# Hybrid gated-attention layer: second branch's factors one stage on, branch sums on VectorE, recurrent values in blocks of 512 columns

## The chip, the cores and the metric

One core of a Trainium2 chip runs the whole layer. The metric is the device time of one execution in microseconds. Engines are named as the profile names them: PE is TensorE (PEld its weight loads), DVE is VectorE, ACT is ScalarE, POOL is GpSimd, SP is SyncE, which here issues transfers.

## The reference

The layer takes x (1024 tokens by 1024 channels, float32) and a conditioning vector c. In short:

```python
mod = silu(c) @ ada_w + ada_b                      # shift, scale, gate
h = rms_norm(x) * (1 + scale) + shift
hq, hf, hi, hz, gq, gk, gv, gz, ga, mg = split(h @ w_in)
y_h = rms_norm(attention(silu(hq), k(hf), hi, log f(hf)), whole width) * silu(hz)
y_g = rms_norm(attention(gq, gk, gv, log_sigmoid(ga @ alpha)/16), per head) * silu(gz)
u_h, u_g = y_h @ w_branch[0], y_g @ w_branch[1]
merged = sigmoid(mg[0]) * u_h + sigmoid(mg[1]) * u_g
out = rms_norm(x + gate * (merged @ w_out))
```

`attention` is causal gated linear attention: a state per head that decays by a gate for each channel. The recurrent branch (HGRN, y_h) has 8 heads of 128 channels, the other (GLA, y_g) 4 heads with 128 key and 256 value channels.

## The kernel before

**Precision.** Every large float32 product is made of three matmuls of a faster type: an operand is split into a high half (cast on ScalarE, L193, L1163, L1182) and a low half (operand less high half on VectorE, L196, L1164, L1183), and high x high, high x low and low x high are summed in PSUM.

**Projections.** A list of jobs runs one after the other (`Stream.go`, L738). `Feat` (L461) makes 128 features of all tokens: 8 steps of 6 matmuls with 512 moving columns. `Vblk` (L480) makes the values of 256 columns: the tokens' tile of h is the stationary operand and 256 columns of weights move, 192 matmuls in 16 steps. The GLA heads come first, then the 8 recurrent heads; before every second of these stands a `Vblk` for two heads. Weights of the next jobs are loaded and split ahead (`ahead`, L721) as far as the 46 buffers of 4 KB a partition allow; the splitting ahead is tried at the fourth step of a job alone.

**Tracks.** After each step, `weave` (L749) advances two queues of side work: `side`, with the attention of one head after the other (L528, which holds TensorE, ScalarE and VectorE steps), and `back`, with preparations for the products. Each entry yields how many steps it wants to wait. On each engine, instructions run in the order in which they stand there.

**Gate side.** `gate_side` (L899) loads the third part of ada_w in eight pieces, sums them on VectorE, each times a value of c (L907, L909), and spreads the sum over the partitions with four full-precision matmuls (L916, L917). It stands in `side`, ahead of the first recurrent head's attention.

**Products.** The last stages (L1287) make four products of 1024 x 1024 x 1024, b = 0 to 3: the two merge gates' columns (b = 0: gate 1, b = 1: gate 0), then the GLA branch (b = 2) and the recurrent branch (b = 3). Each is made block by block with seven instead of eight block products, in the order p = 1, 2, 5, 6, 3, 7, 4 ("groups" below: 48 matmuls each, four pairs of output tiles with 12). That takes sums and differences of blocks, the factors, of h, y_g and y_h. `factors` (L1067) loads four blocks of the activations from memory, subtracts (L1087), and stores the factors to memory, twice. For y_h the blocks are first multiplied by the reciprocal norm (L1081), and all seven are stored. `build` (L1153) loads a group's factor and splits it, `prep_duo` (L1179) does so with the weights of two pairs, two tiles ahead (L1292). ScalarE and VectorE take the results out of PSUM (L1220, L1225, L1229).

**Merging.** `put_gate1` stores the sigmoid of gate 1 to memory (L1316), and `load_gate1` brings it back; `put_t1` multiplies it with u_g. `put_m` (L1334) multiplies gate 0 with u_h and adds the GLA part:

```python
nc.vector.tensor_mul(g, g, ap)
nc.gpsimd.dma_start(g, gate1[d][:, sl], accum_op=ALU.add)
```

The second line is a transfer that adds, issued from POOL. `make_m` (L1346) then splits the sum, leaving the last two halves for later. `OutBlk` (L995) makes the output projection, 16 blocks of 24 matmuls, each taken out of PSUM by VectorE (L1030).

## Time and profile before

| what | us |
|---|---|
| three runs | 1292.81, 1295.80, 1296.76 (median 1295.8) |
| the profiled execution | 1292.4, its span 1290.7 |
| PE busy | 1227.4 |
| DVE busy | 791.7 |
| ACT busy | 505.9 |
| projections and attention | 126 to 844 of the span |
| products b = 0, 1, 2, 3 | 844 to 1190 |
| output projection | 1190 to 1291 |

Times of one profiled execution are counted from the start of its span. A row "x waits for y" gives the time in which an engine had nothing to do and what ended it. Busy times of overlapping instructions are not added twice in a window. A granted clock of 1.00 is TensorE at full speed; 0.50 is half.

### The profile page before, as it was taken

How to read it: one execution, taken by the hardware profiler on the slowest of the kernel's cores; microseconds unless marked ns; L12 is line 12 of the kernel's file. 1: busy time of each engine (PE TensorE's matmuls, PEld its weight loads, DVE VectorE, ACT ScalarE, POOL GpSimd, SP SyncE). 2: the span in 40 equal slices, each digit the busy share in tenths (PEclk: the TensorE clock that was granted, in tenths of full speed). 3: DMA queues.
4: the chain of work that ended last, by engine and by line, in shares of the span. 5: the costliest groups of instructions: out<-in, count | busy, mean ns of one | idle time of the engine just before them, and what ended most of it. 6: DMA issues, size and time to landing. Idle time of an engine off the chain costs nothing. (4 is left out here: it accounts for less than half of the span.)

```text
span 1290.7 us, 21711 instructions
## 1 busy us (share of the span) xinstructions
PE 1227.4 (95%) x8987; PEld 1025.7 (79%) x8987; DVE 791.7 (61%) x1223; ACT 505.9 (39%) x754; POOL 158.9 (12%) x254
## 2 busy tenths in 40 slices
PE   4899999999999989999999999989889999998997
PEld 3767889888898868888987898868678877786785
DVE  5746445877857488677547735676742547547543
ACT  4556522333232423243233222456445555444222
POOL 6500000212113011120110110101210000002000
PEclk9799999999999999999999999999999999998999
DMA  9723342546537375642120221236977546668402
GB/s 281 280 98 99 114 141 89 196 132 212 173 102 253 117 243 184 221 157 58 51 66 18 83 83 49 84 106 226 344 261 269 165 161 199 182 185 212 153 34 98
DMA packets 138485, 199.30 MB, mean 154 GB/s; under 512 B 8075, under 2 KB 102337, under 8 KB 138386
## 3 DMA queue, kind: packets, MB, share of 16 engines
q1 hardware_dynamic: 121314, 144.21, 35.6%
q0 software_dynamic: 17024, 53.70, 11.9%
q8 instruction: 70, 1.15, 0.4%
q14 instruction: 29, 0.24, 0.1%
q10 hardware_dynamic: 48, 0.01, 0.0%
HBM read 140.21 MB, written 53.48 MB: 150 GB/s over the span
## 5 line engine op out<-in xcount | busy, mean ns | idle before, releaser
L455 PE MATMUL pd<-b,b 128*128 128x512 f32 x1632 | 395.9, 396 | 0.0
L455 PEld LDWEIGHTS pd<-b,b 128*128 128x128 f32 x1632 | 301.0, 188 | 62.9 <-issue 0.7
L1242 PE MATMUL pd<-b,b 128*128 128x512 f32 x912 | 223.1, 398 | 17.7 <-ACT b L1182 5.1
L1242 PEld LDWEIGHTS pd<-b,b 128*128 128x128 f32 x912 | 171.4, 191 | 60.8 <-ACT b L1220 7.0
L196 DVE TENSOR_TENSOR b<-b,b 128x1024 fp32r<-128x1024 f32 (+1 forms) x95 | 105.4, 1122 | 81.9 <-ACT b L193 53.5
L514 PE MATMUL pd<-b,b 128*128 128x256 f32 x512 | 150.0, 293 | 0.0
L193 ACT CAST b<-b 128x1024 fp32r<-128x1024 f32 (+1 forms) x95 | 84.7, 905 | 157.4 <-DMA b<-b 25.4
L516 PE MATMUL pd<-b,b 128*128 128x256 f32 x512 | 145.2, 284 | 0.0
L515 PE MATMUL pd<-b,b 128*128 128x256 f32 x512 | 145.0, 283 | 0.0
L1242 PE MATMUL sc_ps<-b,b 128*128 128x512 f32 x432 | 106.8, 393 | 0.1
L1183 DVE TENSOR_TENSOR b<-b,b 128x1024 fp32r<-128x1024 f32 x56 | 67.7, 1219 | 51.5 <-ACT b L1182 34.9
L514 PEld LDWEIGHTS pd<-b,b 128*128 128x128 f32 x512 | 98.1, 192 | 1.3
L515 PEld LDWEIGHTS pd<-b,b 128*128 128x128 f32 x512 | 98.1, 192 | 0.7
L516 PEld LDWEIGHTS pd<-b,b 128*128 128x128 f32 x512 | 98.0, 191 | 0.1
L1242 PEld LDWEIGHTS sc_ps<-b,b 128*128 128x128 f32 x432 | 80.7, 189 | 18.3 <-DVE b L1330 0.5
L1182 ACT CAST b<-b 128x1024 fp32r<-128x1024 f32 x56 | 58.1, 1049 | 41.1 <-DMA gate<-b 8.4
L1164 DVE TENSOR_TENSOR b<-b,b 128x1024 fp32r<-128x1024 f32 x36 | 43.7, 1220 | 35.7 <-ACT b L1163 23.2
L1124 POOL DMA_DIRECT2D ws<-b x64 | 34.7, 543 | 165.5 <-DVE b L1119 70.8
L1163 ACT CAST b<-b 128x1024 fp32r<-128x1024 f32 x36 | 37.7, 1049 | 41.5 <-PE pd L1242 10.1
L702 PE MATMUL pm<-scT,b 128*128 128x128 f32 x256 | 46.9, 275 | 0.0
L634 DVE TENSOR_TENSOR b<-b,tot 128x512 f32<-128x512 f32 x36 | 24.9, 691 | 34.3 <-PE sc_ps L615 15.0
L704 PE MATMUL pm<-b,b 128*128 128x128 f32 x224 | 43.3, 275 | 0.0
(241 smaller groups left out, 1772.9 us busy)
## 6 DMA issues: line engine op xcount, KB each, us to landing
b<-in_w_in_dram SPq DMA_DIRECT2D x66, 512.0 KB, 4.6
ws<-b POOLq DMA_DIRECT2D x64, 256.0 KB, 4.1
b<-ws SPq DMA_DIRECT2D x32, 512.0 KB, 4.4
b<-in_x_dram SPq DMA_DIRECT2D x16, 512.0 KB, 5.7
b<-in_ada_w_dram SPq DMA_DIRECT2D x32, 256.0 KB, 6.0
b<-in_w_branch_dram SPq DMA_DIRECT2D x16, 512.0 KB, 4.9
b<-h SPq DMA_DIRECT2D x14, 512.0 KB, 3.9
b<-yg SPq DMA_DIRECT2D x14, 512.0 KB, 4.6
```

What stands on the lines that cost most here:

```text
L193: i = nc.scalar.copy(hi, src)
L196: (eng or nc.vector).tensor_sub(lo, src, hi.bitcast(F32))
L455: nc.tensor.matmul(ps[0:w, th * 512:(th + 1) * 512], a[:, k, 0:w], b[:, th * 512:(th + 1) * 512], start=(k == 0 and n == 0), stop=(k == KT ...
L514: nc.tensor.matmul(o, lh, hi[:, k % 4, :], start=(k == 0), stop=False)
L515: nc.tensor.matmul(o, lh, lo[:, k % 4, :], start=False, stop=False)
L516: nc.tensor.matmul(o, ll, hi[:, k % 4, :], start=False, stop=(k == KT - 1))
L702: nc.tensor.matmul(o, vch(ch)[:, vh * P:(vh + 1) * P], scT[:, ch, :], start=True, stop=(ch == 0))
L704: nc.tensor.matmul(o, state(ch)[:, vh * P:(vh + 1) * P], q[:, ch * P:(ch + 1) * P], start=False, stop=True)
L1164: nc.vector.tensor_sub(lo, src, hi.bitcast(F32))
L1182: nc.scalar.copy(hi, t)
L1183: nc.vector.tensor_sub(lo, t, hi.bitcast(F32))
L1242: nc.tensor.matmul(o, a[:, sl], c, start=(p in (1, 5) and kt == 0 and n == 0), stop=(kt == 3 and n == 2), skip_group_check=True)
```

## The change

It has five parts.

1. The values of the recurrent heads are made by a new job, `Vblk2`, in two blocks of 512 columns for four heads each. The block stands behind the projections hq and hf of its first head, and that head's attention is started when half of the block is done (`middle`). A head's attention asks for the values when it first needs them (`v = v()`). Weights are split ahead at every second step from the fourth.
2. `gate_side` goes to the rear track, 4 steps after the first block, so behind the weight sums and the GLA factors that stand there, and leaves 3 steps between its last sum and its matmuls.
3. The factors of y_h are begun after p = 2 of b = 1, not at the end of the last head's attention, and their loads are issued from POOL, not SP.
4. `put_m` adds on VectorE, and `make_m` leaves one half for later, not two.
5. `factors` and `weight_sums` wait until 12 buffers are free, not 8 and 6.

```diff
+    class Vblk2:
+        raws, parts = 4, 8
...
+        def run(self):
+            v = [S.get([2, 512]) for _ in range(4)]
+            for g in range(4):
+                if g == 2:
+                    self.middle()
+                ps = dtile()
+                for i in range(2):
+                    t = 2 * g + i
+                    o = ps[:, i * 512:(i + 1) * 512]
+                    for k in range(KT):
+                        hi, lo = self.wt[k // 2]
+                        lh, ll = h_hi[k][:, t * P:(t + 1) * P], h_lo[k][:, t * P:(t + 1) * P]
+                        nc.tensor.matmul(o, lh, hi[:, k % 2, :], start=(k == 0), stop=False)
+                        nc.tensor.matmul(o, lh, lo[:, k % 2, :], start=False, stop=False)
+                        nc.tensor.matmul(o, ll, hi[:, k % 2, :], start=False, stop=(k == KT - 1))
+                        if k % 2:
+                            yield
+                nc.scalar.copy(v[g].rearrange("p a b -> p (a b)"), ps)
...
-                    if u == 3:
+                    if u >= 3 and u % 2:
                         self.ahead(i, loads, preps)
...
             yield 1
+        yield 3
         gate_b[0] = S.get([D])
...
-            stream.back.append([factors(yh_d, f_h, rst), 1])
+            rst_h[0] = rst
+
+    def hgrn_v(h):
+        def done(v):
+            h_state[("v", h // 4)] = v
+            if h == 0:
+                stream.back.append([gate_side(), 4])
+        J.append(Vblk2(C_HI + h * P, done, lambda: start_side(hgrn_attention(h), 4)))
...
-            while len(S.free_list) < 8:
+            while len(S.free_list) < 12:
...
-                nc.sync.dma_start(y[b], part_of(acts, int(b[0]) - 1, int(b[1]) - 1, kk))
+                (nc.sync if mul is None else nc.gpsimd).dma_start(y[b], part_of(acts, int(b[0]) - 1, int(b[1]) - 1, kk))
...
-        while len(S.free_list) < 6:
+        while len(S.free_list) < 12:
...
-        nc.gpsimd.dma_start(g, gate1[d][:, sl], accum_op=ALU.add)
+        nc.vector.tensor_add(g, g, gate1[d][:, sl])
...
-            after(3, p, i, lambda: make_m(2))
+            after(3, p, i, lambda: make_m(1))
...
+    after(1, 2, 3, lambda: stream.back.append([factors(yh_d, f_h, rst_h[0]), 1]))
```

What this moves on the engines, at three places. First TensorE in the values of the recurrent heads; the first block before, and the second block now. Behind the arrow stands first the operand that moves, a half of the weights, and then the stationary one, a tile of h (b_140 and b_148 are the high and low half of one).

```order
L514 MATMUL pd_4782<-b_4507,b_140 128x256
L515 MATMUL pd_4782<-b_4508,b_140 128x256
L516 MATMUL pd_4782<-b_4507,b_148 128x256
L514 MATMUL pd_4782<-b_4507,b_141 128x256
L515 MATMUL pd_4782<-b_4508,b_141 128x256
```

```order
L557 MATMUL pd_5970<-b_5736,b_140 128x512
L558 MATMUL pd_5970<-b_5737,b_140 128x512
L559 MATMUL pd_5970<-b_5736,b_148 128x512
L557 MATMUL pd_5970<-b_5736,b_141 128x512
L558 MATMUL pd_5970<-b_5737,b_141 128x512
```

The same three matmuls for each tile of h now move 512 columns, and there are half as many of them: 384, not 768.

Second, TensorE around the gate side's four matmuls (to pm), before and now. The scores of a head's first step go to sc_ps, the projections' to pd; b_4210 and b_6466 are the sum over the eight pieces.

```order
L455 MATMUL pd_4300<-b_145,b_4247 128x512 x2
L916 MATMUL pm_4308<-b_4210,ones 128x512
L917 MATMUL pm_4308<-b_4211,ones 128x512
L916 MATMUL pm_4312<-b_4210,ones 128x512
L917 MATMUL pm_4312<-b_4211,ones 128x512
L554 MATMUL sc_ps<-xb,b_4101 32x80 x32
```

```order
L597 MATMUL sc_ps<-xb,b_6522 32x80 x32
L455 MATMUL pd_6530<-b_145,b_6478 128x512 x2
L455 MATMUL pd_6530<-b_153,b_6478 128x512 x2
L455 MATMUL pd_6530<-b_145,b_6479 128x512 x2
L963 MATMUL pm_6630<-b_6466,ones 128x512
L964 MATMUL pm_6630<-b_6467,ones 128x512
L963 MATMUL pm_6634<-b_6466,ones 128x512
L964 MATMUL pm_6634<-b_6467,ones 128x512
```

Before, they stand ahead of the first recurrent head's first scores; now behind those of the sixth, six matmuls later.

Third, VectorE in group p = 3 of b = 3, before and now. L1229 (now L1280) takes a block product out of PSUM, L1337 (now L1388) multiplies with gate 0, L1391 is the new addition, L196 makes the low half of the merged sum, L1183 (now L1234) that of weights.

```order
L1229 TENSOR_TENSOR b_10019<-b_10019,pd_7872 128x512
L1183 TENSOR_TENSOR b_10136<-b_10046,b_10135 128x1024
L1337 TENSOR_TENSOR b_8753<-b_8753,b_10019 128x512
L1229 TENSOR_TENSOR b_10019<-b_10019,sc_ps 128x512
L1337 TENSOR_TENSOR b_8769<-b_8769,b_10019 128x512
L1229 TENSOR_TENSOR b_10060<-b_10060,pd_7872 128x512
L1337 TENSOR_TENSOR b_8793<-b_8793,b_10060 128x512
L196 TENSOR_TENSOR b_9898<-b_8753,b_9897 128x512
```

```order
L1388 TENSOR_TENSOR b_8331<-b_8331,b_9639 128x512
L1234 TENSOR_TENSOR b_9754<-b_9666,b_9753 128x1024
L1391 TENSOR_TENSOR b_8331<-b_8331,b_8555 128x512
L1280 TENSOR_TENSOR b_9639<-b_9639,sc_ps 128x512
L196 TENSOR_TENSOR b_9490<-b_8331,b_9489 128x512
L1388 TENSOR_TENSOR b_8345<-b_8345,b_9639 128x512
L1280 TENSOR_TENSOR b_9680<-b_9680,pd_7441 128x512
L1391 TENSOR_TENSOR b_8345<-b_8345,b_8601 128x512
L1388 TENSOR_TENSOR b_8365<-b_8365,b_9680 128x512
L1391 TENSOR_TENSOR b_8365<-b_8365,b_8651 128x512
```

Each multiplication has an addition behind it, and the low half of the sum (L196) follows one multiplication later; before, three multiplications lay between.

More of the change, by code (lines that the diff above doesn't have):

```diff
@@ L522, in run, with __init__, load, prep @@
             self.done(v)
+    class Vblk2:
+        raws, parts = 4, 8
+        def __init__(self, col, done, middle):
+            self.col, self.done, self.middle = col, done, middle
+        def load(self):
+            self.raw = []
+            for kk in range(4):
+                b = S.get([2, 512])
+                nc.sync.dma_start(b, w_in2[kk * 256:(kk + 1) * 256, self.col:self.col + 512].rearrange(
+                    "(k p) f -> p k f", p=P))
+                self.raw.append(b)
+        def prep(self):
+            self.wt = []
+            for b in self.raw:
+                self.wt.append(split(b))
+                S.free(b)
+        def run(self):
[16 more added lines that the diff above has]
+                nc.scalar.copy(v[g].rearrange("p a b -> p (a b)"), ps)
+            for hi, lo in self.wt:
+                S.free(hi, lo)
+            self.done(v)
     def rhs_h(k):
```

27 lines of the change are left out of this document (13 added, 14 removed).

## The prediction

> **What bounds the kernel now.** I read the page first, then the busy time by stage, then what TensorE waited for, and last the timeline around the longest of those waits. The page says which engine is full:
>
> ```profile
> span 1290.7 us, 21711 instructions
> ...
> PE 1227.4 (95%) x8987; PEld 1025.7 (79%) x8987; DVE 791.7 (61%) x1223; ACT 505.9 (39%) x754; POOL 158.9 (12%) x254
> ```
>
> TensorE is busy for 95% of the span. So only two things shorten the run: TensorE instructions that cost less, and waits of TensorE that go. The last five stages of the program, by windows (length, then busy time and instructions of PE, PEld, DVE, ACT and POOL, then granted clock, DMA share and GB/s; they are the products b = 0, 1, 2, 3 and the output):
>
> ```profile
> 844.00:942.70 98.70, 90.32 (x569) 71.99 (x568) 66.91 (x88) 52.54 (x78) 16.63 (x28) 0.98 0.66 227
> 942.70:1023.50 80.80, 77.22 (x337) 62.56 (x336) 35.16 (x35) 40.94 (x56) 2.92 (x6) 1.00 0.69 231
> 1023.50:1103.00 79.50, 77.83 (x337) 62.46 (x336) 47.63 (x52) 40.07 (x50) 0.00 (x0) 1.00 0.58 185
> 1103.00:1190.20 87.20, 80.46 (x338) 64.29 (x338) 51.35 (x61) 42.11 (x57) 12.03 (x14) 0.96 0.67 186
> 1190.20:1290.70 100.50, 89.60 (x385) 72.79 (x383) 44.06 (x74) 26.88 (x56) 1.72 (x2) 0.96 0.29 101
> ```
>
> Stages b = 1, 2 and 3 hold the same 336 matmuls and take 80.8, 79.5 and 87.2 us. The difference is waiting. The list of TensorE's waits names it (us in total, times, longest):
>
> ```profile
> PE pd L1242 <- ACT b L1182: 5.1, 1, 5.1
> PE pd L1242 <- ACT b L1220: 4.8, 3, 2.9
> PE pm L259 <- DVE scT L251: 4.0, 2, 2.2
> PE pm L916 <- DVE b L909: 3.6, 1, 3.6
> PE pm L818 <- DVE b L196: 3.5, 5, 0.8
> PE pd L1242 <- DVE b L1229: 3.4, 2, 2.6
> PE pd L1025 <- DVE xb L1030: 3.1, 2, 2.3
> ```
>
> Of these seven, L259 lies in the start and L818 in the attention, which the change leaves as they are. The other five, 20.0 us, stand where the change works.
>
> **Values in blocks of 512 columns.** Four blocks of 192 matmuls with 256 moving columns become two blocks of 192 with 512. The timeline gives the pitch of both: a run of 111 matmuls of 512 columns, and two of 256 columns between whose starts 45 steps lie:
>
> ```profile
> 450.20 25.33 PE L455 MATMUL pd<-b,b 128*128 128x512 f32 x111
> ...
> 526.77 0.28 PE L516 MATMUL pd<-b,b 128*128 128x256 f32 x1
> ...
> 532.17 0.28 PE L516 MATMUL pd<-b,b 128*128 128x256 f32 x1
> ```
>
> 25.33 / 111 is 0.228 us, the last one's tail included; (532.17 - 526.77) / 45 is 0.120 us. Before, 768 x 0.120 = 92.2 us; now 384 x 0.228 = 87.6 us. That is **-4.6 us** on the path. The Trainium skill, in "TensorE: Matmul & The Clock Gate", section "Back-to-back issue gap", gives an isolated warm matmul its columns over 2.4 GHz and 2.5 ns besides. By that page the 384 matmuls saved are worth 384 x 2.5 ns = 1.0 us, an estimate, and the sum below would be 3.6 us smaller; the two pitches above do not agree with it, since twice 0.120 is 0.012 us more than 0.228. What could take from the 4.6: the four weight tiles of a block are cast and subtracted four steps before it starts, while VectorE also serves a head. Each tile lasts TensorE six matmuls, 1.4 us, so a late tile costs about that; I allow 2 us for both blocks at the far end, and take nothing.
>
> **The gate side moved.** Before, the eight accumulations of the gate bias (L909) run ahead of the first recurrent head, and TensorE meets the four full-precision matmuls (L916, L917) before the last accumulation is there. The timeline row, and then the windows around four places with their granted clock (third value from the end):
>
> ```profile
> 479.09 1.43 PE L916 MATMUL pm<-b,ones 128*128 128x512 f32 x2 [3.56 <-DVE b L909]
> ```
>
> ```profile
> 475.50:490.00 14.50, 10.94 (x76) 4.92 (x76) 11.09 (x15) 3.14 (x5) 1.62 (x3) 0.65 0.39 128
> 926.60:933.50 6.90, 3.94 (x11) 2.54 (x10) 5.29 (x6) 1.76 (x3) 1.63 (x3) 0.77 1.12 353
> 1161.70:1173.00 11.30, 6.16 (x15) 4.36 (x15) 8.92 (x11) 5.54 (x7) 1.72 (x2) 0.70 0.99 265
> 1207.40:1214.00 6.60, 4.28 (x12) 3.23 (x12) 3.05 (x5) 1.45 (x4) 0.00 (x0) 0.74 0.08 32
> ```
>
> A wait costs twice here: TensorE idles 3.56 us, and the clock granted over the 14.5 us around it is 0.65, so (1 - 0.65) x 14.5 = 5.1 us of matmul work is lost as well. Now the accumulations stand in the rear track, spread over two jobs of the sixth head, three steps ahead of the matmuls, and in TensorE's order the matmuls stand behind the sixth head's first scores, whose own vector operations come after the last accumulation in VectorE's order. When TensorE gets there, the accumulation is done. So **-8.7 us**; at the far end 0, if another operation is late there. The 9 transfers and 8 vector operations are the same ones, and the first recurrent head no longer waits behind them.
>
> **The second branch's factors, one stage on.** Before, they run from p = 6 of b = 0 into p = 1 of b = 1. The windows of p = 3, 7, 4 of b = 0 and p = 1 of b = 1, and then of p = 5 and 6 of b = 1, where they will stand (each holds 48 matmuls, which take 48 x 0.228 = 10.9 us):
>
> ```profile
> 904.00:914.90 10.90, 10.90 (x50) 9.03 (x49) 10.11 (x10) 6.73 (x9) 3.22 (x6) 1.00 1.01 327
> 914.90:929.70 14.80, 11.37 (x50) 8.81 (x48) 8.89 (x11) 5.00 (x7) 3.72 (x7) 1.00 0.98 345
> 929.70:942.70 13.00, 12.67 (x48) 9.95 (x49) 5.55 (x6) 5.31 (x8) 3.56 (x8) 0.87 0.92 334
> 942.70:957.80 15.10, 11.52 (x49) 8.86 (x48) 9.52 (x9) 5.44 (x7) 2.92 (x6) 1.00 0.84 297
> ...
> 968.80:979.80 11.00, 11.00 (x50) 8.96 (x49) 3.58 (x3) 5.73 (x9) 0.00 (x0) 1.00 0.58 199
> 979.80:990.70 10.90, 10.90 (x49) 8.90 (x48) 2.45 (x2) 6.32 (x9) 0.00 (x0) 1.00 0.96 333
> ```
>
> The second to fourth rows lose 3.9, 2.1 and 4.2 us, **10.2 us** together, with the DMA engines full (shares of 0.84 to 1.01). VectorE, which makes the low halves of TensorE's operands in order, stands behind the factors' loads:
>
> ```profile
> 938.20 1.23 DVE L1081 TENSOR_TENSOR b<-b,b 128x1024 f32<-128x1024 f32 x1 [5.23 <-DMA b<-yh]
> ```
>
> In the new place VectorE is busy 3 us of 11 instead of 9 to 10, no factor is built for b = 1, and gates are not stored to memory. But the bytes come along: 8 loads and 14 stores of 512 KB are 11.5 MB, or 33 us of the DMA engines at the 345 GB/s of the second row, over seven groups; and p = 6 of b = 1 stands at 333 GB/s already. So some of the stall goes with them. Between nothing and the same 10.2 us again I take half, 5.1, since the operands are prepared two weight tiles, one group, ahead, and the load on VectorE is a third. Net **-5.1 us**. The rear end is +2 (the same stall and some more, as the last head's attention, now two steps later, then lies wholly in b = 0); the near end -10.2.
>
> These loads also go from SP's queue to POOL's. POOL waits there for VectorE's results with its stores, but the four loads of a half are issued before its first store. How quickly POOL's transfers land beside SP's, for the factors themselves (KB each, median us):
>
> ```profile
> fh<-b POOLq DMA_DIRECT2D x14, 512.0 KB, 6.2
> b<-fh SPq DMA_DIRECT2D x14, 512.0 KB, 4.2
> ```
>
> Two microseconds more is inside the six steps (8 us) that are left between load and use. A wider threshold of free buffers (12, not 8 or 6) delays the weight sums, but in the order in which the program is written out they end in the middle of the values of heads 4 to 7, before the products begin; I cost it at nothing; the cover is the projections of the four heads that follow, and without it the first products would wait for their weights.
>
> **Branches added on VectorE.** Before, VectorE multiplies (L1337), POOL issues an adding DMA (L1340), and ScalarE's cast of the sum (L193) waits for the landing. The windows of p = 3, 7, 4 of b = 3, ScalarE's wait, TensorE's wait in the output stage, and an addition of the size of the new one:
>
> ```profile
> 1148.00:1158.90 10.90, 10.90 (x50) 9.03 (x49) 8.57 (x11) 2.37 (x4) 2.53 (x3) 1.00 0.56 152
> 1158.90:1178.10 19.20, 14.06 (x50) 10.57 (x49) 11.55 (x16) 7.67 (x11) 1.76 (x4) 0.82 0.86 229
> 1178.10:1190.20 12.10, 11.17 (x50) 8.94 (x49) 11.55 (x15) 6.26 (x8) 4.28 (x5) 1.00 0.82 185
> ```
>
> ```profile
> 1163.18 0.62 ACT L193 CAST b<-b 128x512 fp32r<-128x512 f32 x1 [8.02 <-DMA b<-b]
> ```
>
> ```profile
> 1209.91 0.59 PE L1025 MATMUL pd<-b,b 128*128 128x512 f32 x1 [2.32 <-DVE xb L1030]
> ```
>
> ```profile
> L1032 DVE TENSOR_TENSOR b<-b,xb 128x512 f32<-128x512 f32 x16 | 11.1, 692 | 0.5
> ```
>
> ScalarE stands 8.02 us for one landing, and behind it in its order stand the casts of the weights (L1182) for which TensorE then waits 5.1 us. The group takes 19.2 us instead of 10.9: **8.3 us**, half clock included. The 2.32 us in the output stage come from the same landings, since the last casts hold VectorE's queue, and the clock of 0.74 over 6.6 us adds 1.7: **4.0 us**. Together 12.3 us go. In exchange VectorE does 16 additions, 11.1 us, 12 of them (8.3 us) in these three groups. There it was busy 8.57 + 11.55 + 11.55 = 31.7 us; now it needs 40.0, and three unhindered groups of TensorE last 32.7. So VectorE becomes the late engine at the end, by 7.3 us. TensorE notices that only where it needs something from VectorE: the last weights' low halves, and in the output stage the eviction of the third block, 17 us after the stage begins (1209.91 - 2.32 - 1190.20). Before, that eviction came 2.32 us too late, with VectorE idle in between for the landings. Of the 7.3 us I take 4 as felt: net **-8.3 us**, between -12.3 and, with the 7.3 felt whole and 4.0 of half clock again, -1.0.
>
> **The sum.** -4.6 - 8.7 - 5.1 - 8.3 = -26.7 us. The profiled execution took 1292.4 us, its span 1290.7 and 1.7 around it; it would come to 1265.7. It lies 3.4 us under the median of the three runs, 1295.8, so against that the forecast is **1269 us**. All near ends give -35.8 (1260), all rear ends -2.6 + 0 + 2 - 1.0 = -1.6 (1294).
>
> **Rivals.** *The stall moves with the factors.* The 11.5 MB find the DMA engines full in b = 1, where p = 6 shows 333 GB/s, and TensorE waits for weights there as it did before: the 5.1 us won are not won and 5 more are lost. For it speaks the DMA share of 0.96; against it, that the group with that share took 10.9 us. -26.7 + 5.1 + 5 = -16.6, or 1279 us. Chance 0.13.
>
> *The gate's wait only moves.* If VectorE is behind when TensorE reaches L916's successor, the 8.7 us are paid again: 1278 us. VectorE's order speaks against it. This is also how the change would fail to do what it says. Chance 0.07.
>
> *Slower: the loads on POOL.* VectorE stands in order before each half's first multiplication. If POOL's loads come so late that VectorE waits longer than TensorE's one prepared group, 10.9 us, the rest is lost twice. To lose the 26.7 us, each half must come 10.9 + 13.4 = 24.3 us late; at 30 us late the time is 1269 + 2 x 19.1 = 1307 us. The longest such wait in the trace is 5.23 us. The Trainium skill, in "SBUF — State Buffer", section "SBUF: two separate sides", says that a DMA from POOL's queue cannot write its descriptors while VectorE runs an operation that takes both memory ports, and so appears blocked; that rule speaks against this part of the change. The 6.2 against 4.2 us above bound what it does here so far. Chance 0.03.
>
> **How the numbers follow.** The forecast holds 0.77: its own range is 1260 to 1277. The range 1257 to 1284 takes in the first two rivals and 3 us of spread below. A measurement of this kernel can tell about 0.3%, 3.9 us, from no change. Faster by more than that needs 1291.9 or less: the forecast and both first rivals, and most of what they give together (-8.0 us): 0.94. Within 0.3%: 0.03. Slower: 0.03, the last rival.
>
> **What would show it.** Right: 512-column matmuls for all recurrent values, at 0.228 us; no wait at L916's successor and no half clock before the products; p = 7 and 4 of b = 0 and p = 1 of b = 1 near 11 to 12 us; p = 7 of b = 3 near 11 to 13 us, with ScalarE's casts waiting for VectorE and not for DMA. Wrong: a new wait of TensorE over 3 us in b = 1 or at the start of b = 2; VectorE without idle time from p = 3 of b = 3 into the output stage with waits of TensorE there over 8 us; waits for the first matmuls of the value blocks.

## The result, and the profile after

The changed kernel took 1283.9 us in the median of five runs (1280.9 to 1287.9), the kernel before 1295.8 beside it: a ratio of 0.9906, with an interval of 0.9878 to 0.9935. That is 12 us faster, where 27 were forecast. The profiled execution took 1281.3 us.

The head of the page of the changed kernel:

```profile
span 1279.6 us, 20905 instructions
...
PE 1219.5 (95%) x8603; PEld 1002.3 (78%) x8603; DVE 802.6 (63%) x1239; ACT 506.3 (40%) x754; POOL 151.4 (12%) x246
```

TensorE has the 384 instructions less that the blocks of 512 columns save, and 7.9 us less to do; its share is what it was. Where the rest went shows by stage, in the windows of the projections, of b = 0, 1, 2, 3 and of the output (columns as in the prediction):

```profile
129.00:837.70 708.70, 698.29 (x6134) 589.52 (x6133) 469.18 (x795) 232.72 (x342) 87.41 (x120) 1.00 0.40 129
837.70:931.40 93.70, 90.55 (x632) 71.83 (x631) 60.58 (x80) 53.42 (x79) 11.91 (x18) 1.00 0.52 166
931.40:1019.30 87.90, 81.17 (x337) 64.79 (x337) 45.39 (x42) 38.47 (x55) 12.26 (x23) 0.96 0.85 292
1019.30:1100.50 81.20, 78.05 (x337) 62.45 (x336) 48.11 (x52) 41.21 (x50) 0.00 (x0) 1.00 0.58 193
1100.50:1182.90 82.40, 77.85 (x338) 62.49 (x337) 58.11 (x73) 42.30 (x58) 0.00 (x0) 1.00 0.48 155
1182.90:1279.60 96.70, 87.71 (x385) 71.63 (x383) 46.62 (x78) 26.66 (x56) 0.00 (x0) 0.97 0.27 102
```

The projections took 718 us and now take 709. b = 0 is 5.0 us shorter, b = 3 4.8 and the output 3.8. But b = 1 went from 80.8 to 87.9 us, and b = 2 from 79.5 to 81.2: the stages that the factors left gained less than those that they entered lost. The remaining 3 us lie in the start, which the change leaves alone; in the profiles of the other kernels below, whose start is the same, it took 125.0 to 128.5 us, so this is mostly spread between executions.

The list of what TensorE waited for, where the change works:

```profile
PE sc_ps L658 <- DVE blk L645: 6.8, 6, 2.5
PE pd L1293 <- ACT pd L1276: 5.3, 3, 3.5
...
PE pd L1293 <- DVE b L1234: 3.3, 2, 1.7
...
PE sc_ps L1293 <- DVE b L1280: 2.1, 1, 2.1
...
PE pd L1076 <- DVE xb L1081: 0.8, 1, 0.8
```

The wait for the gate's sums and the one for a landing in b = 3 are gone, and the output stage's fell from 3.1 to 0.8 us. The attention's third score step (L658, before L615) now waits 6.8 us for VectorE, before 1.8; and there is a new wait for ScalarE's copies into a bank (L1276), the longest of which, 3.5 us, lies in b = 1. In b = 1 TensorE idles 6.7 us in all (87.90 less 81.17), and a clock of 0.96 over 87.9 us takes another 3.5, an estimate. Its groups p = 6, 3 and 7, and then p = 7 and 4 of b = 3:

```profile
964.30:975.90 11.60, 11.21 (x49) 8.94 (x48) 2.47 (x3) 5.29 (x8) 0.54 (x1) 1.00 0.95 353
975.90:993.10 17.20, 13.11 (x50) 10.05 (x49) 10.70 (x11) 6.88 (x10) 3.18 (x6) 0.90 0.97 325
993.10:1008.00 14.90, 12.82 (x50) 10.11 (x49) 8.28 (x10) 4.78 (x7) 2.13 (x4) 0.89 0.98 349
...
1156.40:1169.90 13.50, 11.42 (x49) 8.81 (x48) 12.43 (x18) 6.32 (x9) 0.00 (x0) 1.00 0.75 252
1169.90:1182.90 13.00, 11.26 (x50) 8.97 (x49) 13.00 (x19) 6.37 (x9) 0.00 (x0) 1.00 0.20 55
```

p = 3 and 7 of b = 1 take 17.2 and 14.9 us, not 11. First VectorE's timeline. L1132 multiplies a loaded block of y_h, L1138 subtracts two such blocks, L1234 makes the low half of weights, L1280 takes a block product out of PSUM, subtracting or adding it to another (below: a block difference; there are four in p = 3 and four in p = 7):

```profile
976.74 1.23 DVE L1132 TENSOR_TENSOR b<-b,b 128x1024 f32<-128x1024 f32 x1 [7.55 <-DMA b<-yh]
980.18 2.36 DVE L1234 TENSOR_TENSOR b<-b,b 128x1024 fp32r<-128x1024 f32 x2 [2.21 <-ACT b L1233]
982.45 0.68 DVE L1280 TENSOR_TENSOR b<-b,pd 128x512 f32<-128x512 f32 x1
986.06 1.23 DVE L1132 TENSOR_TENSOR b<-b,b 128x1024 f32<-128x1024 f32 x1 [2.92 <-DMA b<-yh]
987.20 1.22 DVE L1234 TENSOR_TENSOR b<-b,b 128x1024 fp32r<-128x1024 f32 x1
988.34 0.68 DVE L1280 TENSOR_TENSOR b<-b,pd 128x512 f32<-128x512 f32 x1
...
996.93 2.48 DVE L1138 TENSOR_TENSOR b<-b,b 128x1024 f32<-128x1024 f32 x2 [1.44 <-DMA fh<-b]
999.34 0.68 DVE L1280 TENSOR_TENSOR b<-sc_ps,b 128x512 f32<-128x512 f32 x1
```

Then ScalarE (L1233 casts weights, L1371 is the sigmoid of gate 0), and TensorE:

```profile
979.10 1.99 ACT L1233 CAST b<-b 128x1024 fp32r<-128x1024 f32 x2 [4.49 <-DMA b<-in_w_in_dram]
...
981.62 0.59 ACT L1276 COPY pd<-b 128x512 f32<-128x512 f32 x1
...
989.05 0.63 ACT L1371 ACTIVATE b<-b 128x512 f32<-128x512 f32 x1 [4.03 <-DVE b L1280]
989.59 0.58 ACT L1276 COPY pd<-b 128x512 f32<-128x512 f32 x1
```

```profile
982.26 7.35 PE L1293 MATMUL pd<-b,b 128*128 128x512 f32 x24 [3.47 <-ACT pd L1276]
990.22 3.01 PE L1293 MATMUL pd<-b,b 128*128 128x512 f32 x12 [0.61 <-ACT pd L1276]
```

Each time TensorE needs a bank that ScalarE must fill first (L1276). Its longest wait, 3.47 us, leads back to ScalarE alone. The copy at 981.62 stands there behind two casts of weights, and the first of them stood 4.49 us for its load from w_in. In b = 1, p = 3 and 7 take their weights from the stored sums (ws) and p = 4 from w_in, so this cast is for p = 4, two groups on. Its load went out 4.6 us before p = 3 began (971.34 to 975.9), and the cast began 7.8 us after the load went out. VectorE is late for the same reason: its 7.55 us for a factor's load ended at 976.74, within the group's first microsecond, but the low halves ahead of the first difference then waited 2.21 us for those casts.

The wait of 0.61 us at 990.22 is the factors' own. The copy at 989.59 stands behind a sigmoid that waited 4.03 us for a difference, and VectorE made this difference late because it stood 2.92 us at a factor's multiplication whose load had not landed. In p = 7 TensorE waits 2.08 us at 1000.08 for a difference that stands behind two subtractions of the factors, the first of which waited 1.44 us for a store. In VectorE's order of the changed kernel the second half's operations lie between the block differences:

```
974 L1132 TENSOR_TENSOR b_8640<-b_8640,b_7904 128x1024
975 L1234 TENSOR_TENSOR b_8671<-b_8580,b_8670 128x1024
976 L1234 TENSOR_TENSOR b_8622<-b_8538,b_8621 128x1024
977 L1280 TENSOR_TENSOR b_8480<-b_8480,pd_7440 128x512
978 L1132 TENSOR_TENSOR b_8636<-b_8636,b_7904 128x1024
979 L1234 TENSOR_TENSOR b_8717<-b_8625,b_8716 128x1024
980 L1280 TENSOR_TENSOR b_8480<-b_8480,pd_7441 128x512
```

So the first difference of p = 3 is begun 6.5 us after the group's first matmul (982.45 less 975.9); in the kernel before, with no factors there, it was 2.9 us after it.

### The profile page after: what moved, and what is told of

Same layout as the page of the kernel before. It is cut to its first block, busy times and chain, and to the rows that moved or that the text cites. A ratio compares the mean times of both kernels' runs of the same rounds, so it can differ in the third digit from the quotient of the medians.

```text
span 1279.6 us, 20905 instructions
## 1 busy us (share of the span) xinstructions
PE 1219.5 (95%) x8603; PEld 1002.3 (78%) x8603; DVE 802.6 (63%) x1239; ACT 506.3 (40%) x754; POOL 151.4 (12%) x246
## 3 DMA queue, kind: packets, MB, share of 16 engines
q0 software_dynamic: 15872, 53.70, 10.9%
## 5 line engine op out<-in xcount | busy, mean ns | idle before, releaser
L455 PE MATMUL pd<-b,b 128*128 128x512 f32 x1632 | 396.9, 397 | 0.0
L455 PEld LDWEIGHTS pd<-b,b 128*128 128x128 f32 x1632 | 301.1, 189 | 64.1 <-issue 1.2
L1293 PE MATMUL pd<-b,b 128*128 128x512 f32 x912 | 221.7, 395 | 12.6 <-ACT pd L1276 5.3
L1293 PEld LDWEIGHTS pd<-b,b 128*128 128x128 f32 x912 | 170.0, 189 | 55.0 <-ACT pd L1276 6.5
L196 DVE TENSOR_TENSOR b<-b,b 128x1024 fp32r<-128x1024 f32 (+1 forms) x95 | 101.0, 1072 | 69.4 <-ACT b L193 41.7
L193 ACT CAST b<-b 128x1024 fp32r<-128x1024 f32 (+1 forms) x95 | 84.6, 905 | 140.4 <-DMA ws<-b 16.8
L1293 PEld LDWEIGHTS sc_ps<-b,b 128*128 128x128 f32 x432 | 81.2, 190 | 24.0 <-DVE b L1280 2.5
L1234 DVE TENSOR_TENSOR b<-b,b 128x1024 fp32r<-128x1024 f32 x56 | 68.0, 1222 | 45.3 <-ACT b L1233 28.6
L1233 ACT CAST b<-b 128x1024 fp32r<-128x1024 f32 x56 | 58.2, 1049 | 50.0 <-PE pd L1293 14.1
L514 PE MATMUL pd<-b,b 128*128 128x256 f32 x256 | 75.6, 295 | 0.0
L516 PE MATMUL pd<-b,b 128*128 128x256 f32 x256 | 72.5, 283 | 0.0
L515 PE MATMUL pd<-b,b 128*128 128x256 f32 x256 | 72.5, 283 | 0.0
L557 PE MATMUL pd<-b,b 128*128 128x512 f32 x128 | 51.9, 405 | 0.0
L559 PE MATMUL pd<-b,b 128*128 128x512 f32 x128 | 50.2, 392 | 0.0
L558 PE MATMUL pd<-b,b 128*128 128x512 f32 x128 | 50.0, 390 | 0.0
L514 PEld LDWEIGHTS pd<-b,b 128*128 128x128 f32 x256 | 49.0, 191 | 0.5
L515 PEld LDWEIGHTS pd<-b,b 128*128 128x128 f32 x256 | 48.9, 191 | 0.6
L516 PEld LDWEIGHTS pd<-b,b 128*128 128x128 f32 x256 | 48.9, 191 | 0.0
```

The source lines that it names most:

```text
L193: i = nc.scalar.copy(hi, src)
L196: (eng or nc.vector).tensor_sub(lo, src, hi.bitcast(F32))
L455: nc.tensor.matmul(ps[0:w, th * 512:(th + 1) * 512], a[:, k, 0:w], b[:, th * 512:(th + 1) * 512], start=(k == 0 and n == 0), stop=(k == KT ...
L514: nc.tensor.matmul(o, lh, hi[:, k % 4, :], start=(k == 0), stop=False)
L515: nc.tensor.matmul(o, lh, lo[:, k % 4, :], start=False, stop=False)
L516: nc.tensor.matmul(o, ll, hi[:, k % 4, :], start=False, stop=(k == KT - 1))
```

## The experiments

All are times against the kernel before beside them on the same chip, its medians 1296.0 to 1298.0 us. "Steps" are units of six matmuls, in which the tracks count.

| kernel | median us | ratio, interval |
|---|---|---|
| changed (second set) | 1281.9 | 0.9889 (0.9868 to 0.9909) |
| e1 factors' loads on SP | 1279.7 | 0.9865 (0.9845 to 0.9885) |
| e2 and factors in the old place | 1276.9 | 0.9839 (0.9817 to 0.9862) |
| e3 VectorE's addition alone | 1289.3 | 0.9936 (0.9918 to 0.9954) |
| e4 gate side alone | 1293.1 | 0.9964 (0.9946 to 0.9982) |
| e5 e1, gate 1 loaded later | 1281.1 | 0.9887 (0.9867 to 0.9906) |
| e6 e1, old thresholds | 1287.6 | 0.9934 (0.9911 to 0.9956) |
| e7 values alone | 1295.0 | 0.9989 (0.9974 to 1.0004) |
| e8 moved factors alone | 1297.1 | 1.0014 (1.0001 to 1.0027) |
| e10 e1, 20 steps | 1273.0 | 0.9826 (0.9808 to 0.9845) |
| e11 e1, factors before p = 3 | 1282.9 | 0.9901 (0.9884 to 0.9917) |
| e12 thresholds alone | 1308.2 | 1.0098 (1.0083 to 1.0113) |
| e13 e1, both halves' loads ahead | 1280.8 | 0.9874 (0.9852 to 0.9896) |
| e14 changed, 20 steps | 1275.7 | 0.9849 (0.9820 to 0.9879) |
| e15 e10, old values | 1283.8 | 0.9898 (0.9874 to 0.9922) |
| e16 e10, split at one step | 1270.8 | 0.9794 (0.9769 to 0.9819) |
| e17 e1, 30 steps | 1267.9 | 0.9788 (0.9762 to 0.9814) |
| e18 changed, 30 steps | 1269.0 | 0.9795 (0.9768 to 0.9822) |

### The parts undone or alone

**e1**, from the changed kernel:

```diff
-                (nc.sync if mul is None else nc.gpsimd).dma_start(y[b], part_of(...))
+                nc.sync.dma_start(y[b], part_of(...))
```

> The changed kernel with the loads of the second branch's factors issued from SP again, all else as changed. Theory A (the 7.1 us that b = 1 lost come from POOL's order: a half's first load, then a store that waits for VectorE, and only behind it the three other loads; VectorE stands up to 7.5 us for them and the block products behind it hold TensorE): b = 1 falls from 87.9 us to about 82 and the time by 5 to 7 us, to about 1278. Theory B (the DMA engines are full in b = 1, whoever issues): b = 1 stays at 86 to 89 us, the time within 2 us of the changed kernel's 1284.

The time fell by 2 to 4 us against the changed kernel's two sets, with intervals that overlap, and lies between the two theories' times; b = 1 stayed at 86.8, inside theory B's bound, and part of the loss had moved from p = 3 (17.2 to 14.0) to p = 4 (11.4 to 16.8). So the queue is not what makes b = 1 lose.

**e2** is e1 with the factors begun where they were:

```diff
-            rst_h[0] = rst
+            stream.back.append([factors(yh_d, f_h, rst), 1])
...
-    after(1, 2, 3, lambda: stream.back.append([factors(yh_d, f_h, rst_h[0]), 1]))
```

> The changed kernel with the factors of y_h begun at the end of the last head's attention and loaded from SP, as in the kernel before; the other four parts stay changed. If moving the factors lost time (b = 0 to 2 together became 3.9 us longer): this kernel is 2 to 5 us faster than the changed one, 1279 to 1282. If b = 0 to 2 would be worse without the move, since the attention of the last head now ends later: 1286 to 1292, with p = 7 and 4 of b = 0 and p = 1 of b = 1 at 13 to 15 us each.

Faster than the changed kernel's two sets by 5 and 7 us, where 2 to 5 were expected: moving the factors cost time. Against e1, which loads from SP as well, it is 2.8 us, with intervals that overlap. In the old place p = 7 and 4 of b = 0 and p = 1 of b = 1 take 12.7 to 12.9 us, and p = 5 of b = 1 takes 17.1. The other four parts together are worth 0.9839, or 20.9 us.

**e3**, in the kernel before:

```diff
-        nc.gpsimd.dma_start(g, gate1[d][:, sl], accum_op=ALU.add)
+        nc.vector.tensor_add(g, g, gate1[d][:, sl])
...
-            after(3, p, i, lambda: make_m(2))
+            after(3, p, i, lambda: make_m(1))
```

> The kernel before with one part of the change: the branches are added on VectorE, and one half is left for later, not two. The prediction's term was -8.3 us and the two profiles gave -8.6 (b = 3 -4.8, output -3.8): 1287 if it stands by itself. If those 8.6 us came from other parts (weights in time, buffers free): less than 4 us, 1292 or more.

0.9936 is 8.3 us. The window of its b = 3, before 87.2 us:

```profile
1108.60:1191.10 82.50, 77.87 (x338) 62.54 (x337) 58.08 (x73) 42.36 (x58) 0.00 (x0) 1.00 0.48 156
```

**e4**, in the kernel before:

```diff
             yield 1
+        yield 3
         gate_b[0] = S.get([D])
...
-                    start_side(gate_side())
+                    stream.back.append([gate_side(), 4])
```

> The kernel before with one part of the change: the gate side goes to the rear track and leaves three steps before its matmuls. Prediction's term -8.7 us: 1287, with no wait of TensorE before those matmuls and a clock of 1.00 there. Rival: VectorE serves it at the cost of the attention's scores, whose third step then waits (in the changed kernel 6.8 us in six waits): 1290 to 1293.

4.7 us (2.3 to 7.0), between the two: the rival is half right. Of TensorE's waits, for the gate's matmuls none is left, but the scores' third step, 1.8 us in all before, has 4.4, 2.6 more; what else keeps the term from its 8.7 us stays open:

```profile
PE sc_ps L615 <- DVE blk L602: 4.4, 4, 1.5
```

**e7**, the kernel before with `Vblk2`, the deferred `v()` and the splitting at every second step; the start of the gate side is kept ahead of the first head:

```diff
+        def middle():
+            if h == 0:
+                start_side(gate_side())
+            start_side(hgrn_attention(h), 4)
+        J.append(Vblk2(C_HI + h * P, done, middle))
```

> The kernel before with the first part alone: values of the recurrent heads in blocks of 512 columns, splitting ahead at every second step; the gate side still ahead of the first recurrent head. Prediction's term -4.6 us: 1292. By the rule for single matmuls that the prediction set beside it, -1.0: 1295. If the new order of heads also takes the stall at the gate side away or brings waits of the scores, it shows in that profile: 1286 to 1300.

1.4 us, not told from nothing. The projections are 2.2 us shorter (718.1 to 715.9), with the gate's stall still in them (3.0 us) and 4.4 us of waits of the third score step; p = 4 of b = 0 and p = 1 of b = 1 took 15.6 and 18.1 us, before 13.0 and 15.1.

**e8**, the kernel before with the third part alone, the lines of the change's diff for `rst_h`, the loads from POOL and `after(1, 2, 3, ...)`.

> The kernel before with the third part alone: the second branch's factors begun after p = 2 of b = 1, loaded from POOL. Prediction's term -5.1: 1291. If the loss seen when this part is undone in the changed kernel (7 to 9 us) is the part's own: 1300 to 1305, b = 0 shorter by 4 to 8 us and b = 1 longer by 8 to 12.

Its b = 0 and b = 1, before 98.7 and 80.8 us:

```profile
849.30:941.90 92.60, 88.19 (x568) 70.94 (x567) 58.52 (x79) 53.44 (x79) 11.54 (x18) 1.00 0.47 151
941.90:1030.00 88.10, 80.66 (x337) 64.57 (x336) 45.29 (x42) 38.49 (x54) 12.22 (x23) 0.96 0.84 292
```

6.1 us are won and 7.3 lost; with no other part beside it the move costs 1.8 us, less than the 5 to 7 by e2 and the 7 to 9 of the expectation.

**e6** undoes the thresholds in e1, **e12** makes them in the kernel before, by the same lines the other way round:

```diff
-            while len(S.free_list) < 12:
+            while len(S.free_list) < 8:
...
-        while len(S.free_list) < 12:
+        while len(S.free_list) < 6:
```

> The changed kernel with the factors' loads on SP, and the fifth part undone: factors and weight sums begin when 8 and 6 buffers are free, not 12. If the wider threshold moved factors and weight sums onto the heads' second score steps (seven waits for VectorE, 6.8 us, and 1.7 us at half clock): those waits fall under 2 us, the projections by 5 us, the time to about 1275. If these waits come from the new blocks of values and from splitting ahead at every second step: the waits stay at 5 us or more and the time within 2 us of 1280.

> The kernel before with the fifth part alone: factors and weight sums begin when 12 buffers are free. The prediction costed it at nothing: 1296. Undone in the changed kernel it cost 7.9 us, all in the projections (10.0 us longer by the profiles): 1286 to 1290 if it is worth that by itself, with the projections at 708 to 712 us.

Both surprised. In the changed kernel the wider threshold is worth 8 us; in the kernel before it costs 12.7. In e6 the GLA factors run beside the heads, and VectorE stands for one of their loads ahead of a head's first scores, which then come 5.5 us late:

```profile
514.15 1.23 DVE L1138 TENSOR_TENSOR b<-b,b 128x1024 f32<-128x1024 f32 x1 [6.14 <-DMA b<-yg]
```

In e12 it is the gate's sums and the third score step that come late:

```profile
PE sc_ps L615 <- DVE blk L602: 7.5, 4, 2.7
PE pm L916 <- DVE b L909: 5.3, 1, 5.3
```

Its projections took 728.6 us. So the threshold decides beside which heads VectorE's other work falls. I had costed it at nothing. Why the sign turns with the other parts is not settled beyond these waits.

### What in b = 1 is late

**e5** moves gate 1's loads:

```diff
-    for n, d in enumerate(range(8)):
-        after(1, (3, 7)[n // 4], n % 4, lambda d=d: load_gate1(d))
+    for n, d in enumerate((0, 2, 4, 6, 1, 3, 5, 7)):
+        after(*((1, 4), (2, 2))[n // 4], n % 4, lambda d=d: load_gate1(d))
```

> The changed kernel with the factors' loads on SP (1279.7 us by itself) and the eight 512 KB loads of gate 1 taken out of p = 3 and 7 of b = 1: four stand in its p = 4 and four in p = 2 of b = 2. Theory B (the DMA engines are full there: 349 to 397 GB/s in p = 3 and 7 of b = 1; 4.2 MB less): the 9.9 us that b = 1 loses over its seven unhindered groups fall to 3 or less, the time to about 1273. Theory C (VectorE, which gets factors, low halves and block products in one order, is late whatever the DMA engines do): b = 1 stays at 85 to 87 us and the time at 1278 to 1281.

With eight loads of 512 KB (4.2 MB) out of p = 3 and 7 nothing was won:

```profile
932.60:1023.40 90.80, 80.81 (x338) 64.84 (x337) 45.11 (x42) 39.88 (x56) 8.01 (x15) 0.96 0.79 270
```

Their DMA share fell from 1.02 and 1.05 in e1 to 0.87 and 0.67, and they took 17.7 and 12.9 us, in e1 14.0 and 12.0. So full DMA engines alone do not make the loss. Here VectorE's order does it by a detour: it stands 4.50 us at a factor's multiplication; SP stands 5.6 us for one of the low halves behind it, and so issues the load of p = 4's weights 1.9 us before p = 3 begins, not 4.6; ScalarE's cast then stands 6.04 us for that load, ahead of the copy for which TensorE waits 4.88.

**e9** is the changed kernel again.

> The changed kernel itself, unedited, beside the other kernels of this set on one chip. If its ratio to the kernel before is a property of the kernel: 0.988 to 0.993 again, 1280 to 1287 us. If the first set of runs lay high by chance: 0.983 to 0.987, and the loss laid to the moved factors shrinks by the difference.

0.9889: the first set was no accident. In its profile b = 1 is 91.4 us.

**e10** and **e11**, from e1, the first and the second edit:

```diff
-            yield 6
+            yield 6 if mul is None else 20
...
-            while len(S.free_list) < 12:
+            while len(S.free_list) < (12 if mul is None else 8):
...
-    after(1, 2, 3, lambda: stream.back.append([factors(yh_d, f_h, rst_h[0]), 1]))
+    after(0, 7, 3, lambda: stream.back.append([factors(yh_d, f_h, rst_h[0]), 1]))
```

> The changed kernel with the factors' loads on SP and 20 steps, not 6, between a half's loads and its first multiplication. Theory D (VectorE stands in order in front of loads that come later than planned; in the changed kernel 10.5 us in b = 1, with loads on SP 5.0): VectorE's wait for the factors' loads in b = 1 goes to under 1 us, p = 3 and 7 of b = 1 fall to 11 to 12 us each, the time from 1279.7 to about 1275. Theory C (VectorE's own work of 10.5 us in p = 3 is too much beside the block products): the wait goes, but p = 3, 7 or 4 or p = 1 of b = 2 stay 3 us too long wherever the factors fall, the time within 2 us of 1280.

> The changed kernel with the factors' loads on SP and the factors begun four groups earlier, after p = 7 of b = 0, with room asked for 8 buffers: they fall into p = 4 of b = 0 and p = 1, 2, 5 and 6 of b = 1, where no block differences are taken out of PSUM and VectorE is busy 3 to 7 us of 11. Theory C or D: p = 3, 7 and 4 of b = 1 at 11 us each, b = 1 at 78 to 80 us, the time at 1271 to 1274, if nothing comes late in p = 4 of b = 0 and p = 1 of b = 1. Theory B (the DMA engines): their share there is 0.8 to 0.9 already by gate 1's stores, and these groups go to 13 to 15 us each: 1278 to 1283.

e10 gains 6.7 us on e1. Its b = 1:

```profile
930.50:1009.00 78.50, 76.99 (x338) 62.48 (x336) 36.97 (x35) 38.60 (x55) 4.80 (x9) 1.00 0.83 285
```

The loss is gone. Over the whole of b = 1 the DMA engines are as busy as in the changed kernel (0.83 against 0.85), but not where the loss was: the second half's loads now go out 14 to 26 us after p = 3 begins, and the share in p = 3 and 7 is 0.74 and 0.71. So e10 does not set theory B aside. Theory D's times came (p = 3 and 7 at 10.9 and 11.1 us), but not by its reason: it had expected VectorE's waits for these loads to go, and from b = 1 into b = 2 they still come to 8.1 us. What the 20 steps did is to put the second half, loads and operations, behind all eight block differences. In e11, p = 3, 7 and 4 take 10.9, 11.5 and 12.0 us as expected, but p = 1 takes 18.6: there ScalarE stands for loads of weights ahead of a copy that frees a bank (L1271):

```profile
945.24 1.04 ACT L1233 CAST b<-b 128x1024 fp32r<-128x1024 f32 x1 [4.57 <-DMA b<-in_w_in_dram]
946.19 0.59 ACT L1271 ACTIVATE b<-sc_ps 128x512 f32<-128x512 f32 x1
```

It is the stall on ScalarE that p = 3 has in the changed kernel, and b = 1 is no shorter than in e1 (86.7).

**e13**, from e1, issues the second half's loads after the first half's six steps. Now the data is early, and the second half stays ahead of the differences. `load(kk)` holds the loop of four loads:

```diff
             yield 6
+            if mul is not None and kk == 0:
+                while len(S.free_list) < 8:
+                    yield 1
+                load(1)
+            y = ys.pop(kk)
```

> The changed kernel with the factors' loads on SP, and the four loads of the second half issued six steps after those of the first, ahead of the first half's multiplications, when 8 buffers are free. In VectorE's order the second half then stands ahead of every block difference of b = 1, as it does in the changed kernel, but directly behind the first half, and its data should be there. Theory D (late loads in front of VectorE): b = 1 at 78 to 81 us, p = 3 at 11 to 12, the time 1271 to 1275. Theory E (only a place behind the block differences helps, as with 20 steps): b = 1 at 84 us or more, the time 1277 to 1282.

Theory E's bounds: b = 1 is 90.1 us, p = 3 alone 22.9. VectorE waits for the second half's loads 1.4 and 0.5 us only; but a subtraction overwrites a block that a store must have read, and weights come late behind it:

```profile
976.04 5.01 DVE L1149 TENSOR_TENSOR b<-b,b 128x1024 f32<-128x1024 f32 x4 [3.44 <-DMA fh<-b]
980.97 2.35 DVE L1245 TENSOR_TENSOR b<-b,b 128x1024 fp32r<-128x1024 f32 x2
983.24 0.68 DVE L1291 TENSOR_TENSOR b<-b,pd 128x512 f32<-128x512 f32 x1
```

The first difference comes 7.8 us after the group's start. Early loads do not help a factor that stands ahead of the differences.

**e17**, 30 steps, and **e14** and **e18**, the changed kernel, loads on POOL, with 20 and 30 steps as its only edit:

> The fastest kernel so far with 30 steps, not 20, between a half's loads and its first multiplication. In VectorE's order one multiplication of the second half then stands ahead of the block differences of p = 3 of b = 1 again, and the other three far behind them. If a single operation in front of a late load is enough: b = 1 at 82 us or more, 1276 to 1280. If its load is long there by then: b = 1 at 78 us, and p = 4 of b = 1 and p = 1 of b = 2 lose their 3.6 us as well: 1269 to 1272.

> The changed kernel with one number edited: 20 steps, not 6, between a half's loads and its first multiplication, the loads still from POOL. If the place and the lead decide and not the queue: b = 1 at 78 to 82 us and 1272 to 1276, as with SP. If POOL's order (a store that waits for VectorE between a half's first load and the three others) still makes the loads late: b = 1 at 84 us or more, 1278 to 1282.

> The changed kernel with one number edited: 30 steps, not 6, between a half's loads and its first multiplication; the loads stay on POOL. With the loads on SP this took 1267.9 us. If POOL's queue costs nothing once no block difference stands behind a factor operation: 1266 to 1271, b = 1 at 77 to 78 us. If POOL's order delays the loads here too (a store that waits for VectorE between a half's first load and the others): 3 us or more slower, 1271 to 1275, with a wait in p = 1 of b = 2 as with 20 steps (8.2 us there).

The windows of b = 0, 1 and 2 of e17:

```profile
836.40:929.90 93.50, 90.36 (x633) 71.80 (x632) 60.73 (x80) 53.60 (x79) 11.87 (x18) 1.00 0.51 167
929.90:1006.90 77.00, 77.00 (x338) 62.63 (x337) 37.24 (x35) 38.53 (x54) 4.80 (x9) 1.00 0.82 279
1006.90:1085.00 78.10, 77.36 (x338) 62.51 (x337) 53.62 (x57) 41.17 (x50) 3.19 (x6) 1.00 0.74 248
```

b = 1 is TensorE's work without a gap. In p = 3 the DMA engines are full (a share of 1.09 at 355 GB/s, in e18 1.06 at 373, in the changed kernel 0.97 at 325), and the group takes 10.9 us (e18 11.4): this, with e5, is what speaks against theory B. And yet VectorE waits for the factors' loads nearly as long as in the changed kernel (18.2 us in the same stretch); the row of e17:

```profile
DVE b L1132 <- DMA b<-yh: 16.1, 5, 6.5
```

e18's order on VectorE, at the place of the changed kernel's above:

```
971 L1132 TENSOR_TENSOR b_8882<-b_8882,b_7904 128x1024
...
975 L1234 TENSOR_TENSOR b_8607<-b_8531,b_8606 128x1024
976 L1280 TENSOR_TENSOR b_8477<-b_8477,pd_7440 128x512
977 L1280 TENSOR_TENSOR b_8477<-b_8477,pd_7441 128x512
978 L1234 TENSOR_TENSOR b_8648<-b_8571,b_8647 128x1024
979 L1280 TENSOR_TENSOR b_8510<-b_8510,pd_7440 128x512
```

One multiplication stands a group ahead of the differences and none between them. In each kernel with the first difference 2.9 us after the start of p = 3 (before, e2 to e4, e7, e10 to e12, e14 to e18), p = 3 took 10.9 to 11.4 us; in those with 5.0 to 8.4 us (changed, e1, e5, e6, e8, e9, e13), 13.5 to 22.9. ScalarE's order differs in the same way. In e10, e14, e16, e17 and e18 its first copy into a bank (L1276) begins 1.6 us after the group's start, and the cast of p = 4's weights stands behind it; in e17 and e18 this cast waits 1.04 and 1.62 us for its load, at no cost. In the changed kernel, e1, e5, e6, e8 and e9 the cast stands ahead of the copy, which begins 3.0 to 7.1 us after the start.

What the runs leave open: why the second half's place changes the order of cast and copy on ScalarE, and how much is due to its transfers and how much to its operations on VectorE. Every edit that took the operations out of p = 3 took transfers out as well.

e14 has b = 1 at 79.7, but p = 1 of b = 2 at 19.2, where ScalarE stands 5.6 us for a factor of y_g ahead of L1271. With 30 steps POOL costs nothing that can be told (0.9795 against 0.9788).

### The values once more

**e15** is e10 with the first part undone, **e16** e10 with `if u == 3` again.

> The fastest kernel so far (loads on SP, 20 steps; 1273.0 us) with the first part undone: values of the recurrent heads in blocks of 256 columns again, split ahead at the fourth step of a job alone. Prediction's term for these values -4.6 us: 1277 to 1279 here. By what the part gave alone, -1.4 us: 1273 to 1275. If the new blocks also keep VectorE from holding up the scores: 1280 or more.

> The fastest kernel so far (loads on SP, 20 steps; 1273.0 us) with one line undone: weights are split ahead at the fourth step of a job alone, the new values stay. With the values undone as well it took 1283.8 us, its third score steps waiting 11.3 us for VectorE. If it is the splitting at every second step that spreads VectorE's work between the heads' steps: these waits return to 10 us or more, 1280 to 1284. If the splitting is of no account: 1271 to 1275, and the blocks of 512 themselves carry the difference.

The splitting is of no account: e16 is as fast as e10 or a little faster, though its third score steps wait 9.4 us. e15 and e16 differ in the new blocks alone, in their columns and in their place among the heads, which also moves the start of the gate side. Beside the other parts this is worth 13.0 us by the medians, more than the pitches give. The projections of e15 and of e16:

```profile
125.00:850.60 725.60, 708.50 (x6582) 615.97 (x6581) 472.23 (x796) 231.62 (x341) 84.24 (x120) 0.99 0.40 128
```

```profile
126.30:836.80 710.50, 699.62 (x6135) 590.49 (x6134) 469.58 (x795) 232.60 (x342) 87.02 (x120) 1.00 0.40 129
```

TensorE's busy time differs by 8.9 us, the rest is waiting: in e15 one third step stands 5.4 us for VectorE, which has four of the gate's sums, one of them 2.95 us late by its transfer, in front of it.

## Why the prediction was wrong

**The direction and the bound were right**; TensorE's work and waits are what the time is made of.

**The failed step is the factors' term**, -5.1 us: "Between nothing and the same 10.2 us again I take half, 5.1, since the operands are prepared two weight tiles, one group, ahead, and the load on VectorE is a third." b = 0 to 2 together went from 259.0 to 262.8 us, +3.8, past the rear end of +2; by e2 the moved factors, place and queue, cost 5 to 7 us in company, by e8 1.8 alone. The step looked at the groups where the first half falls, p = 5 and 6, and these are indeed unhurt (10.9 and 11.6 us). The second half falls among the block differences of p = 3 and 7, on which ScalarE and TensorE wait, and which p = 5 and 6 do not have. Weights prepared a group ahead protect nothing where a result has to be taken out of PSUM or a bank has to be filled, and here the preparing itself was in the way: the cast of weights that were needed two groups on stood 4.49 us for its load, ahead of the copy for which TensorE waited 3.47. With the second half out of the way (e17) the three stages take 248.6 us, 10.4 less than before: the near end of the term's own bounds.

**The first rival** came nearest (the stall moves along, TensorE waits for weights, 1279 us), and it is half right. The longest wait does hang on weights whose load came late. But its reason, full DMA engines, is not enough: e17 and e18 have them in p = 3 without loss, and e5 loses with a share of 0.87. What counts is what stands behind the late load. **The third rival**, loads on POOL, has at 6 steps a price of 2 to 4 us (e1), far under the 27 that it needed, at 20 steps 2.7 (e14 against e10), and at 30 none that can be told. Whether a POOL transfer had to wait for VectorE's hold on both memory ports to write its descriptors, as the Trainium skill says in "SBUF — State Buffer", section "SBUF: two separate sides", these runs do not tell apart. Blocks of y_h from POOL landed in 7.2 us in the median and from SP in 4.9 at 6 steps, in 6.5 and 5.1 at 30.

**VectorE's addition**, -8.3 us, was right: 8.3 alone, 8.6 by the stages of the changed kernel, p = 7 and 4 of b = 3 at 13.5 and 13.0 us with ScalarE's casts waiting for VectorE.

**The gate side**, -8.7, was half right. No wait and no half clock are left at its matmuls (granted clock 1.00 from 740 to 760). In the changed kernel:

```profile
745.55 1.02 PE L963 MATMUL pm<-b,ones 128*128 128x512 f32 x2
```

But the eight sums now stand among the heads' operations, and the scores wait more: 4.7 us are won alone. The second rival had looked only at L916's successor.

**The values**, -4.6: the pitch holds. Of the changed kernel, the first and the last of 22 matmuls in a row:

```profile
443.06 0.39 PE L559 MATMUL pd<-b,b 128*128 128x512 f32 x1
...
447.85 0.39 PE L559 MATMUL pd<-b,b 128*128 128x512 f32 x1
```

4.79 / 21 is 0.228 us. What they are worth hangs on the waits beside them: 1.4 us alone, 13.0 between e15 and e16.

**The threshold**, costed at nothing, was the second miss: 8 us one way, 12.7 the other. The forecast for values, gate and threshold together, -13.3, is near e2's 20.9 less the addition's 8.3, 12.6 us; but no single one of the three has its forecast size.

The sum itself, 1269 us, is what the changed kernel takes with one number edited (e18, 1269.0, with loads on SP 1267.9). That is partly luck: by b = 0 to 2 the factors give 10.4 us in e17 and 8.6 in e18, not 5.1, and the others do not have their forecast sizes either.

## What to carry to other kernels

When side work is moved, read the order of each engine that it uses behind every instruction that can wait for a transfer, and ask who waits for what stands next; a share of busy time says nothing on that, and a wait of 6 us is free where nothing urgent is queued behind it. Do so for the engines that the side work does not use as well, and follow the longest wait back by name before explaining it: the one in p = 3 led to a cast on ScalarE, not to the factors on VectorE. Put such work behind the operations that take results out of PSUM, not between them, before asking for earlier loads. Price thresholds that steer a scheduler as edits of their own, for all they do is move work.

## What the runs showed of the hardware

Not every wait of TensorE costs clock as well. In the changed kernel, waits of 1.56 and 1.74 us in p = 7 and 4 of b = 3 left the granted clock at 1.00, while those of 3.47 and 2.08 us in b = 1 went with 0.90 and 0.89 over their groups, 1.7 and 1.6 us more. Length alone does not decide it. In the kernel before, the wait of 2.9 us for L1220, in p = 1 of b = 1, left the clock at 1.00 in that group and the next. And one wait, of 2.52 to 2.56 us for L645, stands near 583 us in many of these kernels: the granted clock from 583 to 589 is 0.72 in the changed kernel, e10 and e17, and 1.00 in e2, e11, e13, e16 and e18.

```profile
1000.08 4.61 PE L1293 MATMUL sc_ps<-b,b 128*128 128x512 f32 x12 [2.08 <-DVE b L1280]
...
1162.51 5.32 PE L1293 MATMUL pd<-b,b 128*128 128x512 f32 x22 [1.56 <-DVE b L1234]
...
1175.46 5.30 PE L1293 MATMUL pd<-b,b 128*128 128x512 f32 x22 [1.74 <-DVE b L1234]
```
